# Joint input product of a hybrid diffusion step: heads in pairs, 256-column pieces, each part of a group summed in PSUM and added up afterwards

## The chip, the cores and the metric

One core of a Trainium2 chip runs the whole program. The metric is the device time of one execution in microseconds (us), the median of the runs shown. Matrix products run on TensorE (PE; its weight loads are PEld), elementwise work on VectorE (DVE), ScalarE (ACT) and GpSimd (POOL); SyncE (SP) issues most loads. Sixteen DMA engines move the data between device memory and the on-chip memory SBUF; PE writes only into PSUM, which has eight banks of 512 float32 columns by 128 partitions here.

## The reference, cut to what matters

Two streams of 128 tokens each (context and latent) pass through two trunk layers of width 2048. Layer 0 normalises the tokens, shifts and scales them with `adaLN` vectors (a matrix-vector product with `w_ada`), and multiplies them with `w_in`; the first 3072 columns of the result are queries, keys and values of 8 attention heads, the next 3072 are three streams of a linear recurrence, and the last 448 are its low-rank inputs.

```python
sh1, sc1, g1, sh2, sc2, g2 = split(silu(c) @ w_ada[l] + b_ada[l], 6)
h = rmsnorm(x, norm_g[l, 0]) * (1.0 + sc1) + sh1
proj = h @ w_in                       # 2048 x (3*1024 + 3*1024 + 448)
qa, ka, va, rest = split(proj, [1024, 2048, 3072])
q = qa.reshape(b, t, 8, 2, 64) ...    # 8 heads, two maps of 64; k likewise, v 8 heads of 128
```

Attention, recurrence, output product, ConvFFN, the convolution layer and its ConvFFN follow, and are not touched by the change.

## The kernel before, in words

Every weight matrix is streamed once. A load (SP, issued from `emit_load`, L175) brings a piece of up to 1024 columns by 128 rows into one of 7 `raw` buffers; ACT copies it as the high part (L192) and DVE makes the low part (L194) into one of 4 slots of `wbt`; PE then multiplies three times per 128x128 tile (high by high, high by low, low by high), each time against 256 token columns. The buffers and slots are reused in order, so a load waits until an older piece has been split, and a split waits until PE has used an older slot. The 128 rows of one step are called kt; there are 16.

`gemm_joint` (L273) is the first product of the program, on the 8 heads (groups of q, k, v: 3 tiles of 128 columns, in the matrix 1024 columns apart) and the group "x" (448 columns, 4 tiles). It can't run over all 16 kt in one go, since the `adaLN` vectors of those rows (`sc1`, `sh1`) have to be computed first, from 33.5 MB of `w_ada`. So the 16 kt are cut into five parts of 2, 2, 4, 4 and 4 (`KS`, L388). While one part is multiplied, `fill_joint` (L920) hands out the steps of the `w_ada` product for the next part: loads at L412 and small PE products at L431 (512 KB, 16 products each). `rhs_joint` makes the normalised, modulated rows `hbt` (L582, L585, L587) when a part's vectors are done. The load stream, `w_ada` and `w_in` together, is one queue on SP in the order of the program; PE, DVE and ACT work their lists in order too. A scheduler that models the engines sets these lists when the program is built.

Within a part, the first three heads (`NJ` = 3, `pl`) go piece by piece with 9 products per kt, and their 9 tiles stay in 5 PSUM banks over all five parts. The other five heads and the group x (`pl2`) are held: all pieces of a group are split first, and then each of its tiles is multiplied over the part's rows (L304 to L306), in one of the 2 remaining banks in turn; after each tile ACT (part 0, L309) or DVE (parts 1 to 4, L311) moves its 256 columns from PSUM into or onto the running sum in SBUF. A load of a head's pieces has three runs of 128 columns (512 bytes) per row and kt (L606), two kt to a piece of 768 columns.

After each group of the last part, `in_evac` queues that head's attention (`attn`), of which at most two are active and one step is taken per call of `step_tasks`; attention takes its PSUM banks from the same 7. Then `gemm(p_in, ...)` multiplies the remaining 3072 columns with the same stream (L252, L254, L255), with the rest of the attention in between, and the recurrence follows.

Of the kernel before, what the change touches and what calls it, by code (L numbers as in the profile page):

```python
# [10 lines left out]
F32 = mybir.dt.float32  # L11
# [3 lines left out]
ALU = mybir.AluOpType  # L15
# [4 lines left out]
P = 128  # L20
# [62 lines left out]
def tile_step(ctx: ExitStack, tc: tile.TileContext, A):  # L83
# [189 lines left out]
    def gemm_joint(pls, rhs, evac, sums, fill, steps=2):  # L273


        nts = [len(g["tiles"]) for g in pls[0][0].groups]
        banks = [bank() for _ in range((sum(nts) + 1) // 2)]
        pst = [banks[t // 2][:, (t % 2) * TT:(t % 2) * TT + TT] for t in range(sum(nts))]
        for pi, (pl, pl2) in enumerate(pls):
            last = pi == len(pls) - 1  # L280
            for gi, g in enumerate(pl.groups):
                t0 = sum(nts[:gi])
                for ki, kt in enumerate(pl.kts):
                    r = rhs(kt)
                    w = next_sub()
                    for j, off in enumerate(g["tiles"]):
                        hi, lo = w[:, 0, off:off + P], w[:, 1, off:off + P]
                        ps = pst[t0 + j]
                        pe.matmul(ps, lhsT=hi, rhs=r[:, 0:TT], start=(pi == 0 and ki == 0 and (t0 + j) % 2 == 0),
                                  stop=False, skip_group_check=True)  # L290
                        pe.matmul(ps, lhsT=hi, rhs=r[:, TT:2 * TT], start=False, stop=False, skip_group_check=True)
                        pe.matmul(ps, lhsT=lo, rhs=r[:, 0:TT], start=False, stop=(last and ki == len(pl.kts) - 1),
                                  skip_group_check=True)
                    pump(steps)
                    fill(pi)
                if last:
                    pending.append(evac(gi, g, pst[t0:t0 + nts[gi]]))
            for gi, g in enumerate(pl2.groups):
                rw = [(rhs(kt), next_sub(LA - i, i > 0)) for i, kt in enumerate(pl2.kts)]
                for j, off in enumerate(g["tiles"]):  # L300
                    ps = bank()[:, 0:TT]
                    for i, (r, w) in enumerate(rw):
                        hi, lo = w[:, 0, off:off + P], w[:, 1, off:off + P]
                        pe.matmul(ps, lhsT=hi, rhs=r[:, 0:TT], start=(i == 0), stop=False, skip_group_check=True)  # L304
                        pe.matmul(ps, lhsT=hi, rhs=r[:, TT:2 * TT], start=False, stop=False, skip_group_check=True)  # L305
                        pe.matmul(ps, lhsT=lo, rhs=r[:, 0:TT], start=False, stop=(i == len(rw) - 1),  # L306
                                  skip_group_check=True)
                    if pi == 0:
                        act.activation(sums[gi][j], ps, AF.Copy)  # L309
                    else:  # L310
                        dve.tensor_tensor(out=sums[gi][j], in0=sums[gi][j], in1=ps, op=ALU.add)  # L311
                    pump(steps)
                    fill(pi)
                if last:
                    pending.append(evac(gi, g, sums[gi]))
# [297 lines left out]
    for h in range(HA):  # L613
        g_in.append(grp([h * P, 1024 + h * P, 2048 + h * P], P, [0, P, 2 * P], kind="qkv", h=h))
# [4 lines left out]
    NJ = 3  # L619
    NQ = HA + 1  # L620
    w_in_view = view_for(A["w_in"][0])
    p_joint = [[Plan(w_in_view, gs, list(range(k0, k0 + n))) for gs in (g_in[0:NJ], g_in[NJ:NQ])] for k0, n in zip(K0, KS)]
# [29 lines left out]
    plans.extend([pl for pls in p_joint for pl in pls] + [p_in] + p_outs + p_f0 + [p_p1, p_p2] + p_f1)  # L652
# [46 lines left out]
    def mixer(hb, pjs):  # L699
# [49 lines left out]
        qkvs = [vb[:, 0:3], vb[:, 3:6], kk[:, 4:7]]  # L749
        qkvs += [qkvp.tile([P, 3, TT], F32, name=f"qkv{h}") for h in range(3, HA)]  # L750
        sums = [[qkvs[h][:, j] for j in range(3)] for h in range(NJ, HA)] + [[kk[:, j] for j in range(4)]]
# [114 lines left out]
        def in_evac(gi, g, pst):  # L866
            if g["kind"] == "qkv":
                qkv = qkvs[g["h"]]
                if g["h"] < NJ:
                    for j, ps in enumerate(pst):  # L870
                        act.activation(qkv[:, j], ps, AF.Copy)
                        yield
                tasks.append(attn(g["h"], qkv))
                return
            outs = []
# [939 lines left out]
```

## Time and profile before

| | |
|---|---|
| median of three runs | 2709.16 us (2708.67 to 2729.94) |
| profiled execution, own time | 2707.69 us |
| its span | 2705.6 us |
| granted TensorE clock, mean | 0.977 of full speed |
| PE, DVE, ACT, POOL busy | 97%, 75%, 47%, 11% of the span |
| DMA | 616.59 MB, mean 228 GB/s |
| joint product: first and last matmul | 36.7 and 269.0 us |
| product after it (`p_in`): first matmul | 269.1 us |

The page's rows give busy time by engine and line. A matmul's row lasts longer than its slot on PE, since matmuls are pipelined: what one costs is the step from its start to the next start. The view of windows sums each engine over a stretch and gives the granted clock and the DMA engines' busy share; the view of DMA gives packets, bytes and share by queue; the view of waits says for whom an engine sat idle.

### The profile page before, as it was taken

What the parts mean: (1) busy time and instruction counts of PE and PEld (TensorE: products, weight loads), DVE (VectorE), ACT (ScalarE), POOL (GpSimd) and SP (SyncE); (2) the same over time, 40 slices, a digit from 0 to 9 for tenths busy, and PEclk for the clock granted to TensorE, in tenths of its full rate; (3) what the DMA queues carried; (4) which work ended last, traced back from release to release, by engine and by line L of the source; (5) the groups of instructions that cost most, each with busy time, mean ns of one, the idle gap of its engine ahead of it and who ended that gap; (6) DMA issues with size and microseconds to landing.
All of it is one profiled execution on the core that took longest, in us unless ns stands there. A gap on an engine that the chain in (4) does not pass through costs nothing.

```text
span 2705.6 us, 60522 instructions
## 1 busy us (share of the span) xinstructions
PE 2615.6 (97%) x24347; PEld 2443.4 (90%) x24347; DVE 2020.5 (75%) x3468; ACT 1258.5 (47%) x2074; POOL 298.7 (11%) x313
## 2 busy tenths in 40 slices
PE   6999998999999999999999989999999999999998
PEld 5889996667898999999999989978889999999998
DVE  3457765767579998978999989996479985566655
ACT  3335654554345444434444454346344454355544
POOL 2000012011100000000000047653200000000000
PEclk8999999999799999999999989999999999999999
DMA  9997656655356887877878857865798876666653
GB/s 293 304 272 209 204 169 217 243 193 199 129 189 195 257 268 240 286 249 247 277 247 267 274 169 246 275 229 177 243 299 277 258 234 195 195 195 193 194 190 119
DMA packets 446969, 616.59 MB, mean 228 GB/s; under 512 B 33461, under 2 KB 317464, under 8 KB 446048
## 3 DMA queue, kind: packets, MB, share of 16 engines
q1 hardware_dynamic: 442288, 600.83, 70.2%
q0 software_dynamic: 3040, 6.57, 0.7%
q10 hardware_dynamic: 1360, 5.33, 0.5%
q8 instruction: 191, 3.13, 0.5%
q14 instruction: 90, 0.74, 0.1%
HBM read 604.75 MB, written 7.86 MB: 226 GB/s over the span
## 4 chain that ended last, share of the span: by engine, by line
PE 84%; DVE 7%; DMA 6%; ACT 1%; issue 1%; SPq 0%; POOL 0%; DVEq 0%; ACTq 0%; POOLq 0%
PE mm L255 22%; PE mm L252 22%; PE mm L254 22%; PE ada L431 4%; DVE cu L1655 3%; DMA raw<-in_w_ada 2%; DMA raw<-in_w_in 2%; PE mm L1087 1%; DVE wbt L194 1%; DMA raw<-in_w_up 1%; PE mm L304 1%; PE mm L306 1%; PE mm L305 1%; PE mm L1648 1%; PE mm L1120 1%
## 5 line engine op out<-in xcount | busy, mean ns | idle before, releaser
L192 ACT ACTIVATE wbt<-raw 128x1024 fp32r<-128x1024 f32 (+3 forms) x768 | 793.7, 1037 | 1035.4 <-PE mm L254 696.8
L252 PE MATMUL mm<-hbt,wbt 128*128 128x256 f32 x3888 | 1086.5, 282 | 6.0 <-ACT hbt L585 2.3
L254 PE MATMUL mm<-hbt,wbt 128*128 128x256 f32 x3888 | 1081.5, 280 | 2.7 <-DVE hbt L587 2.7
L194 DVE TENSOR_TENSOR wbt<-raw,wbt 128x1024 fp32r<-128x1024 f32 (+1 forms) x688 | 812.6, 1188 | 357.7 <-ACT wbt L192 345.5
L255 PE MATMUL mm<-hbt,wbt 128*128 128x256 f32 x3888 | 1064.2, 280 | 3.5 <-DVE wbt L194 3.3
L252 PEld LDWEIGHTS mm<-hbt,wbt 128*128 128x128 f32 x3888 | 733.3, 189 | 20.3 <-issue 9.2
L254 PEld LDWEIGHTS mm<-hbt,wbt 128*128 128x128 f32 x3888 | 734.0, 189 | 6.9 <-DVE hbt L587 4.7
L255 PEld LDWEIGHTS mm<-hbt,wbt 128*128 128x128 f32 x3888 | 723.2, 189 | 9.7 <-DVE wbt L194 4.7
L254 PE MATMUL mm<-u,wbt 128*128 128x256 f32 x1344 | 371.0, 278 | 0.0
L252 PE MATMUL mm<-u,wbt 128*128 128x256 f32 x1344 | 370.9, 278 | 0.0
L255 PE MATMUL mm<-u,wbt 128*128 128x256 f32 x1344 | 365.7, 278 | 0.0
L456 DVE SCALAR_TENSOR_TENSOR av<-raw,silu_c,av 128x1024 f32<-128x1024 f32 x270 | 337.2, 1278 | 29.6 <-DMA raw<-in_w_ada 29.5
L194 POOL TENSOR_TENSOR wbt<-raw,wbt 128x1024 fp32r<-128x1024 f32 x80 | 193.5, 2427 | 909.8 <-DMA raw<-in_w_pw 800.2
L252 PEld LDWEIGHTS mm<-u,wbt 128*128 128x128 f32 x1344 | 252.2, 188 | 0.4 <-issue 0.4
L254 PEld LDWEIGHTS mm<-u,wbt 128*128 128x128 f32 x1344 | 252.0, 188 | 0.4 <-issue 0.4
L255 PEld LDWEIGHTS mm<-u,wbt 128*128 128x128 f32 x1344 | 249.1, 188 | 0.4 <-issue 0.4
L431 PE MATMUL ada<-raw,silu_c 128*32 128x256 f32 (+2 forms) x2688 | 166.0, 337 | 31.3 <-DMA raw<-in_w_ada 15.6
L1655 DVE SCALAR_TENSOR_TENSOR cu<-mm,vec,cu 128x256 f32<-128x256 f32 x428 | 174.4, 470 | 2.2 <-ACT cu L1639 1.0
L1544 DVE SCALAR_TENSOR_TENSOR cv<-mm,vec,cv 128x254 f32<-128x254 f32 x344 | 147.3, 474 | 11.8 <-ACT cv L1539 11.8
L431 PEld LDWEIGHTS ada<-raw,silu_c 128*32 128x32 f32 x2688 | 70.3, 112 | 91.7 <-issue 26.2
L304 PE MATMUL mm<-hbt,wbt 128*128 128x256 f32 x304 | 91.7, 302 | 1.9 <-DVE qkv L311 1.0
L1539 ACT ACTIVATE cv<-mm,vec 128x256 f32<-128x256 f32 x172 | 72.0, 474 | 45.9 <-PE mm L255 45.8
(449 smaller groups left out, 2889.6 us busy)
## 6 DMA issues: line engine op xcount, KB each, us to landing
raw<-in_w_ada SPq DMA_DIRECT2D x384, 512.0 KB, 5.3
raw<-in_w_up SPq DMA_DIRECT2D x688, 256.0 KB, 4.2
raw<-in_w_down SPq DMA_DIRECT2D x168, 512.0 KB, 5.0
raw<-in_w_pw SPq DMA_DIRECT2D x128, 256.0 KB, 4.3
raw<-in_w_in SPq DMA_DIRECT2D x128, 192.0 KB, 6.1
raw<-in_w_in SPq DMA_DIRECT2D x48, 512.0 KB, 3.9
raw<-in_w_out SPq DMA_DIRECT2D x32, 512.0 KB, 4.0
raw<-in_w_pw SPq DMA_DIRECT2D x32, 512.0 KB, 4.7
```

Source lines behind the costliest of these rows:

```text
L192: act.activation(w[:, 0, 0:na * n], v, AF.Copy)
L194: pl.lo(pl.count).tensor_tensor(out=w[:, 1, 0:na * n], in0=v, in1=w[:, 0, 0:na * n].bitcast(F32), op=ALU.subtract)
L252: pe.matmul(ps, lhsT=hi, rhs=r[:, 0:TT], start=(ki == 0 and (nl > 0 or j % 2 == 0)), stop=False, skip_group_check=True)
L254: pe.matmul(ps, lhsT=hi, rhs=r[:, TT:2 * TT], start=False, stop=False, skip_group_check=True)
L255: pe.matmul(ps, lhsT=lo, rhs=r[:, 0:TT], start=False, stop=(ki == nk - 1), skip_group_check=True)
L304: pe.matmul(ps, lhsT=hi, rhs=r[:, 0:TT], start=(i == 0), stop=False, skip_group_check=True)
L305: pe.matmul(ps, lhsT=hi, rhs=r[:, TT:2 * TT], start=False, stop=False, skip_group_check=True)
L431: pe.matmul(ps[32 * j:32 * j + 32, 0:nb * 32], lhsT=silu_c[:, kt, :], rhs=rv[:, j], start=(kt == 0), stop=(kt == KT - 1))
L456: dve.scalar_tensor_tensor(out=av[:, s], in0=raw, scalar=sc, in1=av[:, s], op0=ALU.mult, op1=ALU.add)
L1539: act.activation(o, ps, AF.Copy, scale=w(1, ct))
L1544: dve.scalar_tensor_tensor(out=o[:, :, a_], in0=v2(ps)[:, :, b_], scalar=w(k, ct), in1=o[:, :, a_], op0=ALU.mult, op1=ALU.add)
L1655: dve.scalar_tensor_tensor(out=o, in0=pads[a](k), scalar=V("w_dw", k * KT + ct), in1=o, op0=ALU.mult, op1=ALU.add)
```

## The change

Heads are taken in pairs: a group is q, k and v of two heads, 3 runs of 256 columns (1 KB), 768 columns and 6 tiles; a piece holds one kt of such a group instead of two kt of one head. There are 4 pairs and the group x, all treated alike. A group takes 3 banks (x takes 2), is multiplied kt by kt over the part's rows with 18 products per piece, and at the part's end its banks are copied by ACT (part 0) or added by DVE (parts 1 to 4) in whole banks of 512 columns, except that heads 2 and 3 go in halves of 256, because their sums lie in different buffers. The heads' sums are laid out anew (two neighbouring heads side by side for q, for k and for v), and no tile stays in PSUM from part to part. `fill_joint` is called twice per piece, and its rate is set to that count. Two heads' attention is queued when a pair is done.

```diff
-    def gemm_joint(pls, rhs, evac, sums, fill, steps=2):
-        nts = [len(g["tiles"]) for g in pls[0][0].groups]
-        banks = [bank() for _ in range((sum(nts) + 1) // 2)]
-        pst = [banks[t // 2][:, (t % 2) * TT:(t % 2) * TT + TT] for t in range(sum(nts))]
-        for pi, (pl, pl2) in enumerate(pls):
-            last = pi == len(pls) - 1
+    def gemm_joint(pls, rhs, evac, sums, fill, steps=1):
+        for pi, pl in enumerate(pls):
             for gi, g in enumerate(pl.groups):
-                t0 = sum(nts[:gi])
+                nt = len(g["tiles"])
+                banks = [bank() for _ in range(nt // 2)]
                 for ki, kt in enumerate(pl.kts):
                     r = rhs(kt)
                     w = next_sub()
                     for j, off in enumerate(g["tiles"]):
                         hi, lo = w[:, 0, off:off + P], w[:, 1, off:off + P]
-                        ps = pst[t0 + j]
+                        ps = banks[j // 2][:, (j % 2) * TT:(j % 2) * TT + TT]
...
+                        if j in (nt // 2 - 1, nt - 1):
+                            pump(steps)
+                            fill(pi)
-            for gi, g in enumerate(pl2.groups):
-                rw = [(rhs(kt), next_sub(LA - i, i > 0)) for i, kt in enumerate(pl2.kts)]
-                for j, off in enumerate(g["tiles"]):
-                    ps = bank()[:, 0:TT]
...
-                    if pi == 0:
-                        act.activation(sums[gi][j], ps, AF.Copy)
-                    else:
-                        dve.tensor_tensor(out=sums[gi][j], in0=sums[gi][j], in1=ps, op=ALU.add)
-                    pump(steps)
-                    fill(pi)
+                for bk_, parts in zip(banks, sums[gi]):
+                    o = 0
+                    for t in parts:
+                        n = t.shape[-1]
+                        src = bk_[:, o:o + n]
+                        o += n
+                        if pi == 0:
+                            act.activation(t, src, AF.Copy)
+                        else:
+                            dve.tensor_tensor(out=t, in0=t, in1=src, op=ALU.add)
+                if pi == len(pls) - 1:
+                    pending.append(evac(gi, g, [t for parts in sums[gi] for t in parts]))
...
-    for h in range(HA):
-        g_in.append(grp([h * P, 1024 + h * P, 2048 + h * P], P, [0, P, 2 * P], kind="qkv", h=h))
+    for h in range(0, HA, 2):
+        g_in.append(grp([h * P, 1024 + h * P, 2048 + h * P], 2 * P, [P * j for j in range(6)], kind="qkv", h=h))
...
-    NJ = 3
-    NQ = HA + 1
+    NQ = HA // 2 + 1
...
-                qkv = qkvs[g["h"]]
-                if g["h"] < NJ:
-                    for j, ps in enumerate(pst):
-                        act.activation(qkv[:, j], ps, AF.Copy)
-                        yield
-                tasks.append(attn(g["h"], qkv))
+                tasks.extend(attn(h, qkvs[h]) for h in (g["h"], g["h"] + 1))
...
-                    want = (seen[pi][0] * 8 * KS[pi + 1]) // (NJ * KS[pi] + 19)
+                    want = (seen[pi][0] * 8 * KS[pi + 1]) // (2 * NQ * KS[pi])
```

What this does to the engines' lists is shown at three places. The first is SP's queue in the second half of the joint product (`raw` is the load buffer). Before:

```order
L606 DMA raw<-in_w_in 128x3x128 x2
L412 DMA raw<-in_w_ada 128x2x512 x2
L606 DMA raw<-in_w_in 128x3x128 x2
L412 DMA raw<-in_w_ada 128x2x512 x2
L606 DMA raw<-in_w_in 128x3x128 x2
```

and now:

```order
L402 DMA raw<-in_w_ada 128x2x512 x2
L596 DMA raw<-in_w_in 128x3x256
L402 DMA raw<-in_w_ada 128x2x512
L596 DMA raw<-in_w_in 128x3x256
L402 DMA raw<-in_w_ada 128x2x512 x2
L596 DMA raw<-in_w_in 128x3x256 x2
```

One issue of 384 KB stands where two of 192 KB stood; the mix of `w_ada` and `w_in` and its order stay much the same.

The second is PE around the last product of `w_ada` for this stage (`ada`; `mm` is a PSUM bank, `hbt` the rows, `wbt` the split weights). Before:

```order
L304 MATMUL mm_2421<-hbt_380,wbt_98 128x256
L431 MATMUL ada_2205<-raw_2384,silu_c_77 32x128 x8
L305 MATMUL mm_2421<-hbt_380,wbt_98 128x256
L306 MATMUL mm_2421<-hbt_380,wbt_98 128x256
L304 MATMUL mm_2421<-hbt_380,wbt_98 128x256
L305 MATMUL mm_2421<-hbt_380,wbt_98 128x256
L306 MATMUL mm_2421<-hbt_380,wbt_98 128x256
L304 MATMUL mm_2435<-hbt_380,wbt_98 128x256
```

and now:

```order
L289 MATMUL mm_2251<-hbt_381,wbt_98 128x256
L421 MATMUL ada_2181<-raw_2358,silu_c_77 32x128 x8
L286 MATMUL mm_2249<-hbt_381,wbt_98 128x256
L288 MATMUL mm_2249<-hbt_381,wbt_98 128x256
L289 MATMUL mm_2249<-hbt_381,wbt_98 128x256
L286 MATMUL mm_2249<-hbt_381,wbt_98 128x256
L288 MATMUL mm_2249<-hbt_381,wbt_98 128x256
L289 MATMUL mm_2249<-hbt_381,wbt_98 128x256
L286 MATMUL mm_2250<-hbt_381,wbt_98 128x256
```

The three lines of a tile's products are now L286, L288 and L289, and each bank comes back for every kt of the group. Of the 1344 products of the joint stage 485 stood behind this last `w_ada` product before, and 474 do now.

The third is DVE in the fourth part (rows of `wbt` are splits of pieces, the others add a bank of PSUM to a sum). Before:

```order
L194 TENSOR_TENSOR wbt_98<-raw_2259,wbt_98 128x768
L311 TENSOR_TENSOR qkv3_444<-qkv3_444,mm_2264 128x256
L311 TENSOR_TENSOR qkv3_444<-qkv3_444,mm_2288 128x256
L311 TENSOR_TENSOR qkv3_444<-qkv3_444,mm_2312 128x256
L194 TENSOR_TENSOR wbt_98<-raw_2336,wbt_98 128x768
L194 TENSOR_TENSOR wbt_98<-raw_2341,wbt_98 128x768
```

and now:

```order
L194 TENSOR_TENSOR wbt_98<-raw_2252,wbt_98 128x768
L194 TENSOR_TENSOR wbt_98<-raw_2294,wbt_98 128x768
L194 TENSOR_TENSOR wbt_98<-raw_2336,wbt_98 128x768
L194 TENSOR_TENSOR wbt_98<-raw_2368,wbt_98 128x768
L303 TENSOR_TENSOR qkv4_445<-qkv4_445,mm_2249 128x512
L303 TENSOR_TENSOR qkv4_445<-qkv4_445,mm_2250 128x512
```

Adds now come once per group and part, in whole banks. Here three pieces of the next pair (2294, 2336 and 2368) are split ahead of them. Over the 19 ends of groups at which another follows in this stage, two or three later pieces stand split ahead of the first add at 17, and one at 2.

## Rows read from the trace of the kernel before

**Rows 1.** The page, part 1: busy us (share of the span) xinstructions.
```profile
PE 2615.6 (97%) x24347; PEld 2443.4 (90%) x24347; DVE 2020.5 (75%) x3468; ACT 1258.5 (47%) x2074; POOL 298.7 (11%) x313
```

**Rows 2.** Windows of 0 to 450 us; the columns are named in the first row.
```profile
core 0: us, PE busy (x) PEld busy (x) DVE busy (x) ACT busy (x) POOL busy (x), PEclk, DMA share, GB/s
36.00:200.00 164.00, 156.76 (x1893) 134.73 (x1883) 77.49 (x166) 51.58 (x88) 0.00 (x0) 0.97 0.94 289
...
210.00:220.00 10.00, 10.00 (x88) 9.84 (x87) 5.58 (x10) 3.04 (x4) 0.00 (x0) 1.00 0.65 177
200.00:269.00 69.00, 65.27 (x526) 62.99 (x527) 54.51 (x130) 38.85 (x86) 4.99 (x8) 0.98 0.72 207
269.00:427.00 158.00, 158.00 (x1341) 154.30 (x1343) 100.61 (x190) 84.08 (x166) 21.35 (x51) 1.00 0.62 181
```

**Rows 3.** DMA of 36 to 200 us: queue's packets, MB, share of 16 engines; issues.
```profile
q1 hardware_dynamic: 51455, 47.12, 93.7%
...
raw<-in_w_ada SPq DMA_DIRECT2D x53, 512.0 KB, 6.3
raw<-in_w_in SPq DMA_DIRECT2D x84, 192.0 KB, 6.5
```

**Rows 4.** DMA of 210 to 220 us, heads' pieces alone.
```profile
q1 hardware_dynamic: 3550, 1.74, 64.2%
...
raw<-in_w_in SPq DMA_DIRECT2D x10, 192.0 KB, 3.3
```

**Rows 5.** DMA of 2350 to 2400 us, the second layer's `w_up` alone.
```profile
q1 hardware_dynamic: 10045, 9.68, 63.8%
...
raw<-in_w_up SPq DMA_DIRECT2D x38, 256.0 KB, 3.2
```

**Rows 6.** DMA of 2500 to 2550 us, the same loads.
```profile
q1 hardware_dynamic: 11384, 9.54, 63.4%
```

**Rows 7.** PE timeline about the last `w_ada` product: start us, us, engine, instruction.
```profile
199.08 0.28 PE L304 MATMUL mm<-hbt,wbt 128*128 128x256 f32 x1
199.29 0.65 PE L431 MATMUL ada<-raw,silu_c 128*32 128x128 f32 x16
199.86 0.39 PE L305 MATMUL mm<-hbt,wbt 128*128 128x256 f32 x1
```

**Rows 8.** PE timeline at the end of the joint product.
```profile
268.90 0.28 PE L305 MATMUL mm<-hbt,wbt 128*128 128x256 f32 x1
269.01 0.28 PE L306 MATMUL mm<-hbt,wbt 128*128 128x256 f32 x1
269.12 0.28 PE L252 MATMUL mm<-hbt,wbt 128*128 128x256 f32 x1
```

**Rows 9.** PE waits, 36 to 270 us: us in total, times, longest us.
```profile
PE ada L431 <- DMA raw<-in_w_ada: 5.3, 3, 2.6
PE mm L816 <- DVE a L810: 3.6, 1, 3.6
PE mm L304 <- DVE qkv L311: 1.0, 2, 0.7
PE mm L304 <- ACT qkv L309: 0.5, 1, 0.5
```

**Rows 10.** DVE lines by form, 0 to 270 us: count, busy us, mean ns, idle before.
```profile
L194 DVE TENSOR_TENSOR wbt<-raw,wbt 128x768 fp32r<-128x768 f32 x64 | 60.5, 954 | 61.6 <-ACT wbt L192 59.7 <-DMA raw<-in_w_in 1.9
L311 DVE TENSOR_TENSOR qkv<-qkv,mm 128x256 f32<-128x256 f32 x60 | 24.4, 415 | 26.1 <-PE mm L306 25.8
...
L1504 DVE COPY kb<-mm 128x512 f32<-128x512 f32 x4 | 2.6, 680 | 0.0
...
L371 DVE COPY vec<-mm 128x256 f32<-128x256 f32 x2 | 0.8, 398 | 0.0
```

**Rows 11.** PE timeline at the one long gap behind 200 us.
```profile
238.09 0.28 PE L306 MATMUL mm<-hbt,wbt 128*128 128x256 f32 x1
241.99 0.45 PE L816 MATMUL mm<-table,a 128*128 128x128 f32 x1 [3.62 <-DVE a L810]
...
244.15 0.41 PE L304 MATMUL mm<-hbt,wbt 128*128 128x256 f32 x1
244.37 0.41 PE L305 MATMUL mm<-hbt,wbt 128*128 128x256 f32 x1
```

More of the change, by code (lines that the diff above doesn't have):

```diff
@@ L287, in gemm_joint @@
                         hi, lo = w[:, 0, off:off + P], w[:, 1, off:off + P]
-                        ps = pst[t0 + j]
-                        pe.matmul(ps, lhsT=hi, rhs=r[:, 0:TT], start=(pi == 0 and ki == 0 and (t0 + j) % 2 == 0),
-                                  stop=False, skip_group_check=True)
+                        ps = banks[j // 2][:, (j % 2) * TT:(j % 2) * TT + TT]
+                        pe.matmul(ps, lhsT=hi, rhs=r[:, 0:TT], start=(ki == 0 and j % 2 == 0), stop=False,
+                                  skip_group_check=True)
@@ L291, in gemm_joint @@
                         pe.matmul(ps, lhsT=hi, rhs=r[:, TT:2 * TT], start=False, stop=False, skip_group_check=True)
-                        pe.matmul(ps, lhsT=lo, rhs=r[:, 0:TT], start=False, stop=(last and ki == len(pl.kts) - 1),
+                        pe.matmul(ps, lhsT=lo, rhs=r[:, 0:TT], start=False, stop=(ki == len(pl.kts) - 1),
                                   skip_group_check=True)
-                    pump(steps)
-                    fill(pi)
-                if last:
-                    pending.append(evac(gi, g, pst[t0:t0 + nts[gi]]))
@@ L298, in gemm_joint @@
-            for gi, g in enumerate(pl2.groups):
-                rw = [(rhs(kt), next_sub(LA - i, i > 0)) for i, kt in enumerate(pl2.kts)]
-                for j, off in enumerate(g["tiles"]):
-                    ps = bank()[:, 0:TT]
[L302 to L307, printed above, removed]
-                    if pi == 0:
-                        act.activation(sums[gi][j], ps, AF.Copy)
-                    else:
-                        dve.tensor_tensor(out=sums[gi][j], in0=sums[gi][j], in1=ps, op=ALU.add)
[L312 to L315, printed above, removed]
+                        if j in (nt // 2 - 1, nt - 1):
+                            pump(steps)
+                            fill(pi)
@@ L618, in tile_step @@
             g_in.append(grp([j0 + q * 512], 512, [0, P, 2 * P, 3 * P], kind=nm, c=4 * q))
-    NJ = 3
-    NQ = HA + 1
+    NQ = HA // 2 + 1
     w_in_view = view_for(A["w_in"][0])
-    p_joint = [[Plan(w_in_view, gs, list(range(k0, k0 + n))) for gs in (g_in[0:NJ], g_in[NJ:NQ])] for k0, n in zip(K0, KS)]
+    p_joint = [Plan(w_in_view, g_in[0:NQ], list(range(k0, k0 + n))) for k0, n in zip(K0, KS)]
     p_in = Plan(w_in_view, g_in[NQ:], list(range(KT)))
@@ L651, in tile_step @@
     stream["stop"] = len(g_in) * KT
-    plans.extend([pl for pls in p_joint for pl in pls] + [p_in] + p_outs + p_f0 + [p_p1, p_p2] + p_f1)
+    plans.extend(p_joint + [p_in] + p_outs + p_f0 + [p_p1, p_p2] + p_f1)
     def v2(ap):
@@ L748, in mixer @@
         vec_task = [vectors()]
-        qkvs = [vb[:, 0:3], vb[:, 3:6], kk[:, 4:7]]
-        qkvs += [qkvp.tile([P, 3, TT], F32, name=f"qkv{h}") for h in range(3, HA)]
-        sums = [[qkvs[h][:, j] for j in range(3)] for h in range(NJ, HA)] + [[kk[:, j] for j in range(4)]]
+        flat = lambda ap: ap.rearrange("p a t -> p (a t)")
+        twos = [vb[:, 0:6]] + [qkvp.tile([P, 6, TT], F32, name=f"qkv{h}") for h in (4, 6)]
+        ones_ = [kk[:, 4:7], qkvp.tile([P, 3, TT], F32, name="qkv3")]
+        sums = [[[flat(t[:, 2 * j:2 * j + 2])] for j in range(3)] for t in twos]
+        sums.insert(1, [[t[:, j] for t in ones_] for j in range(3)])
+        sums.append([[flat(kk[:, 2 * j:2 * j + 2])] for j in range(2)])
+        twos = [t.rearrange("p (m h) t -> p m h t", h=2) for t in twos]
+        qkvs = [twos[0][:, :, 0], twos[0][:, :, 1]] + ones_ + [twos[1 + i // 2][:, :, i % 2] for i in range(4)]
         tasks = []
@@ L867, in in_evac @@
             if g["kind"] == "qkv":
-                qkv = qkvs[g["h"]]
-                if g["h"] < NJ:
-                    for j, ps in enumerate(pst):
-                        act.activation(qkv[:, j], ps, AF.Copy)
-                        yield
-                tasks.append(attn(g["h"], qkv))
+                tasks.extend(attn(h, qkvs[h]) for h in (g["h"], g["h"] + 1))
                 return
+            if g["kind"] == "x":
+                pst = [kk[:, j] for j in range(4)]
             outs = []
```

## The prediction

> **What bounds the kernel now.** The page's first part comes first: PE is busy for 97% of the span [rows 1], so a change that only moves work off other engines gains little, and the question is where PE waits or stands in for a wait. The change touches the joint product alone, so the next view is the table of windows around it [rows 2]. The reader is to see two stretches with different limits. From 36 us, where the first joint product starts, to 200 us the DMA engines are busy for 94% of the time at 289 GB/s; PE's 157 of 164 us busy are not PE at its peak, because a lone matmul's row is longer than its slot. From 200 to 269 us the DMA share drops to 0.72 and PE does 526 instructions in 65.3 of 69 us; it is behind and catches up. The stretch from 269 to 427 us, the rest of the input product, has PE busy throughout: whatever the joint product ends earlier, that stretch starts earlier, and nothing in it takes the time back.
>
> The timeline tells what separates the two stretches [rows 7]: the last `w_ada` product of the stage runs at 199.3 us, and behind it PE has 485 joint products to do by the order of its list. They end at 269.1 us [rows 8]. One product costs 10.00 / 88 = 0.114 us where PE has nothing else [rows 2], so 485 cost 55.3 us; the other 14 us are attention's products and one long gap [rows 11]. So the end of the joint product is (arrival of the last `w_ada` piece, set by DMA) + (products behind it, set by PE). I cost the change in these two terms.
>
> **Term 1, DMA up to 200 us.** The bytes are the same. What changes is the run: 512 bytes per packet become 1 KB. Before, the heads' pieces alone (210 to 220 us) moved 1.74 MB at a share of 64.2% [rows 4], which is 1.74 MB / (10 us x 0.642) = 271 GB/s per full share. The later `w_up` loads have just the form that the change gives to the heads, runs of 256 columns, with 9.68 MB in 10045 packets: 9.68 / (50 x 0.638) = 303 [rows 5], and again 9.54 / (50 x 0.634) = 301 GB/s [rows 6]. In 36 to 200 us there are 84 issues of 192 KB, 16.5 MB [rows 3]: 61 us of all 16 engines at 271, 55 us at 302. That is 6 us less work for a resource that is busy for 93.7% of the stretch [rows 3], and I take all of it: -6.0. Its ends are 0, if packets overlap so that the stretch moves at the same rate, and -16: the 6 us, and the 10 us (6.3% of 164) in which the DMA engines stood idle because the load queue waited for buffers.
>
> [...]
>
> **Term 2, PE behind the last `w_ada` product.** By the new order 474 joint products stand behind it instead of 485: 11 x 0.114 = -1.3 us. The number of heads whose attention is complete at the end of the joint product stays at two; one more head gets as far as its scores there, and that work leaves the next stretch, which is PE's as well: 0.
>
> **Banks.** Before, only two banks were left for the held groups, and PE waited for the evacuation: 1.0 us for DVE and 0.5 us for ACT [rows 9]. Now three banks of a group are emptied while a whole next group (36 or 72 products, 4.1 or 8.2 us) runs, and seven banks hold two groups. These waits go: -1.5; ends 0 and -1.5.
>
> **Adds and copies.** DVE had 76 adds of 256 columns at 415 ns [rows 10]: 31.5 us. Now it has 24 of these and 44 of 512. The trace has no such add; a copy from PSUM takes 398 ns for 256 columns and 680 for 512 [rows 10], so I take 415 + 280 = 0.69 us (ends 0.415 and 0.83, twice the short one). That makes 10.0 + 30.4 = 40 us, 9 us more. DVE is busy for 77 of 164 and 54 of 69 us [rows 2]; of the 9 us 2 fall into the last part. Beside idle time they cost 0, and without that cover 9. ACT's copies out of PSUM grow and shrink by a few us at 52 of 164 us busy: 0.
>
> **Issues and fill.** SP makes 64 issues fewer; its queue waits for buffers, not for itself: 0. The `w_ada` steps keep their pace (18 steps are due at 22.5 of 40 calls, where it was 17.4 of 31).
>
> **The gap at 238 us.** PE waited 3.6 us for attention's weights `a`, and the twelve products behind it went at half the clock, 0.22 us apart [rows 11]: about 5 us in all. In the new list the same transposes stand 72 products behind the scores, but two heads share DVE and ACT on the way. I expect a wait of like size: 0; ends -5 and +4, a second such wait.
>
> **Sum.** -6.0 - 1.3 - 1.5 = -8.8 us. The profiled execution took 2707.7 us; it would take 2698.9. The median of the runs is 2709.2, 1.5 more, so on it I forecast 2700 us.
>
> **The rivals.**
>
> *No gain on DMA.* If the packets' cost is hidden between the 16 engines, or the memory behind them is the limit (from 36 to 200 us 47.1 MB moved at 93.7%, which is 307 GB/s per full share with both sizes mixed [rows 3]), term 1 is 0. For it: the mixed stretch is no slower than `w_up` alone. Against: more than half of its bytes are 2 KB runs. It gives 2709.2 - 2.8 = 2706 us. [...]
>
> *Everything closes up.* The held groups kept two of four slots until their last tile; now each slot comes free after 18 products. If that also fills the DMA engines' idle 10 us, and the gap at 238 us goes, the sum is -16 - 1.3 - 1.5 - 5 = -24: 2685 us. For it: PE waited 5.3 us for `w_ada` [rows 9] while the load queue stood still. Against: the queue's order has hardly changed.
>
> *Slower: the adds stand in front of the splits.* DVE works in order. An add waits until PE ends a group, and with it every split behind it; a group's adds take 3 x 0.69 us and the next split 0.95 [rows 10], 3.0 us in all, against 19 x 0.415 spread over a part before. One split piece gives PE 18 x 0.114 = 2.05 us of work. It decides at 3.0 / 2.05 = 1.5 pieces ahead: with one, PE stands still for about 1 us at each of 20 ends, +19 - 8.8 = 2719 us; with none, +60 - 8.8 = 2760. The list has two or three at 17 of 19 ends, which speaks against; for it speaks that a split there is only in the list, and its piece may be late.
>
> The other way in which the change could fail to do what it says, runs that are cut to 512 bytes anyway, is excluded by the packets of `w_up` (964 bytes on average [rows 5]).
>
> **How the numbers follow.** Forecast 0.50, no gain on DMA 0.22, everything closes 0.16, slower 0.12. The likeliest case alone spans 2693 to 2704. The range reaches from 2684, one below the third case's value, to 2712, three above the median, and leaves out most of the slower case and the far tail of the third. 1% is 27 us, about what a measurement of this kernel can tell from no change. Under 2682 lies only a part of the third case, if the first 36 us gain too: 0.07. Over 2736 lies the slower case with hardly any piece ahead: 0.05. The rest, 0.88, is no change by that measure.
>
> **What would show it.** Term 1: the last `w_ada` product at about 193 us instead of 199.3, and the heads' loads alone at about 300 GB/s per full share. Term 2: about 69 us from it to the end of the joint product, less 1 to 3. Banks: no PE wait on L301 or L303. The slower rival: PE waits for L194 at the ends of groups, with L303 just before it on DVE. The forecast is wrong if the next stretch, 158 us before, changes by more than 3 us, or if the recurrence behind it, whose lists were built anew, moves by itself.

## The result, and the profile after

The changed kernel takes 2694.4 us (median of 20 runs, 2690.9 to 2710.6), the kernel before beside it 2718.1 us (20 runs, 2701.9 to 2740.4). The ratio is 0.991, with a 95% interval of 0.989 to 0.9931: a gain of 0.7 to 1.1%, about what a measurement of this kernel can tell from no change. The forecast was 2700, from 2684 to 2712.

The runs of the kernel before fall into two groups (9 of 2701.9 to 2709.8 us, 11 of 2716.5 to 2740.4), those of the changed one lie within 6 us in 19 of 20 cases, with one at 2710.6. Lower group against lower group it is 2705.2 against 2694.4 us, and the two profiled executions, 2707.7 and 2696.3, stand as far apart: 11 us, and it is these 11 that the traces can explain. The rest of the 24 us between the medians is how often the upper group comes; the last section returns to it.

The page after, first part, as [rows 1]:

```profile
PE 2599.1 (96%) x24347; PEld 2436.0 (90%) x24347; DVE 2031.0 (75%) x3460; ACT 1258.8 (47%) x2063; POOL 300.5 (11%) x313
```

The windows of [rows 2], now:

```profile
36.00:200.00 164.00, 161.32 (x2019) 143.89 (x2020) 99.80 (x199) 63.47 (x104) 0.00 (x0) 0.98 0.96 316
200.00:269.00 69.00, 63.22 (x497) 60.52 (x496) 53.32 (x127) 38.28 (x89) 6.21 (x10) 0.95 0.63 187
269.00:427.00 158.00, 153.47 (x1299) 147.41 (x1297) 97.43 (x184) 80.61 (x154) 28.09 (x66) 1.00 0.61 175
```

The gain shows in the first one: 316 GB/s where it was 289, and 126 more PE instructions in the same 164 us. Its DMA, to set beside [rows 3]:

```profile
q1 hardware_dynamic: 38576, 51.45, 95.2%
...
raw<-in_w_ada SPq DMA_DIRECT2D x53, 512.0 KB, 6.0
raw<-in_w_in SPq DMA_DIRECT2D x51, 384.0 KB, 5.8
```

There are a quarter fewer packets, 4.3 MB more, and a share of busy time that is hardly higher. It looks as if the longer runs had done it. The heads' pieces alone (200 to 210 us, [rows 4]) speak against that:

```profile
q1 hardware_dynamic: 1777, 1.74, 62.8%
```

1.74 MB / (10 us x 0.628) = 277 GB/s per full share, against 271 before and some 300 forecast. The timeline at the last `w_ada` product and at the end of the joint product (L252 is the next stretch's first), as [rows 7, 8], and at attention's transposes, as [rows 11]:

```profile
185.97 0.64 PE L421 MATMUL ada<-raw,silu_c 128*32 128x128 f32 x16
...
231.46 0.30 PE L810 MATMUL mm<-table,a 128*128 128x128 f32 x1
232.63 0.44 PE L810 MATMUL mm<-table,a 128*128 128x128 f32 x2 [0.88 <-DVE a L804]
237.85 0.45 PE L810 MATMUL mm<-table,a 128*128 128x128 f32 x1 [4.78 <-DVE a L804]
...
259.38 0.28 PE L252 MATMUL mm<-hbt,wbt 128*128 128x256 f32 x1
```

And the PE waits from 36 to 270 us, as [rows 9]:

```profile
PE ada L421 <- DMA raw<-in_w_ada: 10.6, 4, 9.2
PE mm L810 <- DVE a L804: 5.7, 2, 4.8
PE mm L286 <- ACT hbt L575: 0.4, 1, 0.4
PE mm L288 <- DVE hbt L577: 0.3, 1, 0.3
```

(The 9.2 us lie ahead of the first joint product.) The last `w_ada` product comes 13.3 us earlier, the stretch behind it is 3.6 us longer (73.4 where it was 69.8), and the remaining 2435 us of the span are 1.5 shorter: together the 11. (Two more traces of the kernel before, below, divide these 11 otherwise.)

### The profile page after: what moved, and what is told of

Read it like the earlier page. It is cut to its first block, busy times and chain, and to the rows that moved or that the text cites. A ratio compares the mean times of both kernels' runs of the same rounds, so it can differ in the third digit from the quotient of the medians.

```text
span 2694.4 us, 60352 instructions
## 1 busy us (share of the span) xinstructions
PE 2599.1 (96%) x24347; PEld 2436.0 (90%) x24347; DVE 2031.0 (75%) x3460; ACT 1258.8 (47%) x2063; POOL 300.5 (11%) x313
## 4 chain that ended last, share of the span: by engine, by line
PE 80%; DVE 5%; DMA 3%; ACT 1%; issue 1%; POOL 1%; SPq 1%; DVEq 0%; ACTq 0%; POOLq 0%
PE mm L252 22%; PE mm L255 22%; PE mm L254 22%; PE ada L421 3%; DMA raw<-in_w_ada 2%; PE mm L1078 1%; DMA raw<-in_w_up 1%; DVE cu L1646 1%; DVE wbt L194 1%; PE mm L1639 1%; PE mm L1111 1%; DVE av L446 1%; PE mm L1115 0%; PE ada L454 0%; PE mm L1273 0%
## 5 line engine op out<-in xcount | busy, mean ns | idle before, releaser
L252 PE MATMUL mm<-hbt,wbt 128*128 128x256 f32 x3888 | 1087.5, 282 | 6.0 <-ACT hbt L575 2.3
L254 PE MATMUL mm<-hbt,wbt 128*128 128x256 f32 x3888 | 1082.3, 280 | 3.2 <-DVE hbt L577 3.2
L194 DVE TENSOR_TENSOR wbt<-raw,wbt 128x1024 fp32r<-128x1024 f32 (+1 forms) x688 | 814.0, 1189 | 351.8 <-ACT wbt L192 343.1
L255 PE MATMUL mm<-hbt,wbt 128*128 128x256 f32 x3888 | 1065.1, 281 | 5.5 <-DVE wbt L194 5.3
L252 PEld LDWEIGHTS mm<-hbt,wbt 128*128 128x128 f32 x3888 | 734.3, 189 | 20.6 <-issue 9.2
L252 PE MATMUL mm<-u,wbt 128*128 128x256 f32 x1344 | 371.1, 278 | 0.0
L194 POOL TENSOR_TENSOR wbt<-raw,wbt 128x1024 fp32r<-128x1024 f32 x80 | 193.8, 2431 | 908.5 <-ACT wbt L192 905.7
L252 PEld LDWEIGHTS mm<-u,wbt 128*128 128x128 f32 x1344 | 252.2, 188 | 0.4 <-issue 0.4
L421 PE MATMUL ada<-raw,silu_c 128*32 128x256 f32 (+2 forms) x2688 | 157.3, 338 | 31.6 <-DMA raw<-in_w_ada 25.2
L286 PE MATMUL mm<-hbt,wbt 128*128 128x256 f32 x448 | 131.6, 298 | 0.4 <-ACT hbt L575 0.4
L288 PE MATMUL mm<-hbt,wbt 128*128 128x256 f32 x448 | 127.1, 285 | 0.3 <-DVE hbt L577 0.3
```

The source lines that it names most:

```text
L194: pl.lo(pl.count).tensor_tensor(out=w[:, 1, 0:na * n], in0=v, in1=w[:, 0, 0:na * n].bitcast(F32), op=ALU.subtract)
L252: pe.matmul(ps, lhsT=hi, rhs=r[:, 0:TT], start=(ki == 0 and (nl > 0 or j % 2 == 0)), stop=False, skip_group_check=True)
L255: pe.matmul(ps, lhsT=lo, rhs=r[:, 0:TT], start=False, stop=(ki == nk - 1), skip_group_check=True)
L286: pe.matmul(ps, lhsT=hi, rhs=r[:, 0:TT], start=(ki == 0 and j % 2 == 0), stop=False, skip_group_check=True)
L421: pe.matmul(ps[32 * j:32 * j + 32, 0:nb * 32], lhsT=silu_c[:, kt, :], rhs=rv[:, j], start=(kt == 0), stop=(kt == KT - 1))
```

## The experiments

The stretch up to the last `w_ada` product gained twice what I had given the longer runs. Four things had changed at once: the length of the runs, the slots that a held group kept, the pace of the `w_ada` steps, and the three heads that lay in PSUM over all parts. Each was taken by itself. "w_ada" and "joint" are the start of the last `w_ada` product and of the first product behind the joint ones, in us of the one trace; "layer" is the time from the start of the first product of the second layer's `w_down` to that of the last one. Each ratio is to the runs of the kernel before that were taken beside that kernel (their medians are 2714.6 to 2722.6 us in the series e1 to e10); it is not the quotient of two medians of the table.

| kernel | median us (runs) | ratio to before, 95% | w_ada | joint | layer |
|---|---|---|---|---|---|
| before, three traces | 2718.1 (20) | | 199.3, 195.8, 195.2 | 269.1, 265.8, 265.5 | 464.0 each |
| changed | 2694.4 (20) | 0.991, 0.989 to 0.9931 | 186.0 | 259.4 | 464.0 |
| e1 runs of 512 bytes | 2696.5 (7) | 0.9925, 0.9889 to 0.9961 | 186.0 | 259.6 | 464.0 |
| e2 single heads | 2693.5 (12) | 0.9912, 0.9886 to 0.9938 | 183.0 | 248.7 | 464.0 |
| e3 transposes later | 2690.3 (12) | 0.9918, 0.9885 to 0.9951 | 185.1 | 243.6 | 464.0 |
| e4 four heads | 2716.6 (12) | 0.9993, 0.997 to 1.0015 | 180.0 | 254.6 | 481.9 |
| e5 single, slots held | 2687.7 (10) | 0.9904, 0.9866 to 0.9942 | 185.6 | 251.7 | 464.0 |
| e6 before, six slots | 2737.7 (4) | 1.0108, 1.0047 to 1.0169 | 194.5 | 275.5 | 481.9 |
| e7 before, even pace | 2715.4 (10) | 1.0029, 0.9986 to 1.0072 | 197.3 | 269.3 | 464.0 |
| e8 before, none held | 2700.2 (10) | 0.9945, 0.9914 to 0.9976 | 185.0 | 249.7 | 481.9 |
| e9 as e5, transposes later | 2690.6 (12) | 0.9924, 0.989 to 0.9957 | 185.7 | 246.1 | 464.0 |
| e10 as e8, two banks left | 2729.7 (10) | 1.0051, 1.0009 to 1.0093 | 204.3 | 283.8 | 481.9 |

The cause is read from the columns w_ada and joint. The medians mix in the last column, which has two values 18 us apart, in code that no edit touches; what picks the value is not known.

**The runs.** In the changed kernel a piece is fetched by head:

```
+            if g.get("kind") == "qkv":
...
+                for i in range(2):
+                    eng.dma_start(out=d4[:, i], in_=s4[:, :, i * P:(i + 1) * P])
+                return
...
-        g_in.append(grp([h * P, 1024 + h * P, 2048 + h * P], 2 * P, [P * j for j in range(6)], kind="qkv", h=h))
+        g_in.append(grp([h * P, 1024 + h * P, 2048 + h * P], 2 * P, [(j % 2) * 384 + (j // 2) * P for j in range(6)], kind="qkv", h=h))
```

> The changed kernel with one thing undone: a pair's piece of 128x768 is fetched in two transfers of 192 KB with runs of 128 columns (512 bytes), one for each head, into a slot that holds the heads one behind the other. Loop order, sums, adds and slots stay. Theory A, the length of the runs: the load rate in the stretch that DMA limits falls back from 329 to about 304 GB/s per full DMA share (100 to 150 us), the last w_ada product comes at about 198 us instead of 186, the joint product ends at about 270 us instead of 259, and the time is about 2705 us, 11 above the changed kernel. Theory B, the structure (a part's group is finished before the next begins, so slots come free evenly): the last w_ada product stays at 186 to 188 us and the time at 2694 to 2697 us.

The DMA of 36 to 200 us and the last `w_ada` product of this kernel:

```profile
q1 hardware_dynamic: 58961, 51.48, 102.0%
...
raw<-in_w_in SPq DMA_DIRECT2D x102, 192.0 KB, 6.1
```

```profile
185.99 0.64 PE L421 MATMUL ada<-raw,silu_c 128*32 128x128 f32 x16
```

Half as many packets again, twice the issues of the heads, and the same bytes in the same time to 0.1%: theory A is out. The share of busy time rose from 95.2 to 102.0% and the last `w_ada` product started at 185.99 us against 185.97, so the share was not a measure of room left. That is what had misled me.

**Loop order and pairs.** The new `gemm_joint` with the old groups (`for h in range(HA)`, pieces of 128 columns, two rows a slot):

> The new loop order alone: heads one at a time as before (pieces of 128 columns, two rows of a head in a slot, runs of 512 bytes, adds of 512 and 256 columns), but every head goes through PSUM part by part and none is held over the parts. Theory A, the length of the runs: as before the change, last w_ada product at about 198 us, joint product to about 270 us, time about 2706 us. Theory B, the structure: last w_ada product at 186 to 188 us and about 2695 us. If the first experiment keeps the gain and this one loses it, it is the pairs' slot (one row of six tiles instead of two rows of three) and not the runs.

183.0 us with runs of 512 bytes: the gain needs neither the pairs nor the runs. The joint product even ends 10.7 us earlier than in the changed kernel, but the profiled execution, 2699.9 us, is 3.6 longer. Its windows (columns as in [rows 2]) show why:

```profile
560.00:570.00 10.00, 10.00 (x141) 7.11 (x140) 7.60 (x20) 6.51 (x17) 1.05 (x3) 0.77 0.46 164
570.00:580.00 10.00, 10.00 (x66) 6.54 (x61) 1.79 (x4) 2.08 (x3) 0.53 (x2) 0.50 0.22 59
580.00:590.00 10.00, 10.00 (x65) 8.43 (x64) 3.96 (x11) 3.33 (x5) 0.52 (x1) 0.50 0.59 206
590.00:600.00 10.00, 10.00 (x86) 6.25 (x84) 6.81 (x25) 6.34 (x17) 1.17 (x4) 0.87 0.48 162
```

In the recurrence the granted clock fell to 0.50 in this execution, by the four means for about 27 us; the lead was gone: from the first product behind the joint ones to the first of `w_out` this execution took 459.7 us, the changed kernel's 443.4. The traces of before and after show 1.00 in all four windows; a stretch at half clock comes later in both, with a mean of 0.57 from 680 to 720 us before and of 0.66 from 660 to 710 us after. Of e2's 12 runs the profiled one shows the lowest mean clock, 0.974, so this loss need not be in its median, 2693.5 us.

**Four heads to a group**, 512 columns and one transfer of 512 KB for each of q, k and v:

> The change carried on: q, k and v of four heads are a group each, 512 columns in one run of 2 KB, two rows in a slot, one transfer of 512 KB for a slot. Theory A, a cost per packet: if 1 KB runs brought 13 us against 512 bytes, 2 KB runs bring half as much again, 5 to 7 us; the last w_ada product at about 180 us and the time about 2688 us. Rival A2, nothing beyond 1 KB: 186 us and about 2694 us. Rival B, the structure: slots come free after 24 products and two rows, as with single heads before, so that DMA idles more: 188 to 192 us and about 2698 us. Attention starts later in the last part (four heads at a time); I cost that at nothing, since the next stretch covers it.

The 180.0 us that theory A named came, and yet e1 speaks against the runs as its source, and so does e2: product 672 of 1344, half of the joint ones, starts at 147.2 us here and at 148.1 with single heads and 512 bytes (151.0 in the changed kernel, 162 to 167 before). Of the 28 us by which this execution is longer than the changed kernel's, about 10 had been lost by the end of the recurrence, which begins 5 us earlier here but stands at half clock for some 22 us longer (59 us against 37, by the means of the windows of 434 to 715 us), and 18 in the second layer, the last column. The same window of the second layer in this kernel and in the changed one:

```profile
2300.00:2350.00 50.00, 50.00 (x427) 50.00 (x426) 23.57 (x26) 19.10 (x18) 0.00 (x0) 1.00 0.58 184
```

```profile
2300.00:2350.00 50.00, 50.00 (x444) 50.00 (x443) 26.95 (x35) 19.12 (x18) 0.00 (x0) 1.00 0.63 192
```

427 products in 50 us against 444, at a granted clock of 1.00 in both.

**The slots.** First, single heads with a group's products tile by tile over its rows, as before for five heads and x:

```
-                for ki, kt in enumerate(pl.kts):
-                    r = rhs(kt)
-                    w = next_sub()
-                    for j, off in enumerate(g["tiles"]):
+                rw = [(rhs(kt), next_sub(LA - i, i > 0)) for i, kt in enumerate(pl.kts)]
+                for j, off in enumerate(g["tiles"]):
+                    ps = banks[j // 2][:, (j % 2) * TT:(j % 2) * TT + TT]
+                    for ki, (r, w) in enumerate(rw):
```

> Single heads, part by part through PSUM, as in the second experiment, with one thing put back: a group's products go tile by tile over the part's rows, so that its two slots of four stay in use until its last tile (as the kernel before did for five heads and x; here all nine groups). Theory B1, held slots: with two of four slots held, DVE's split of the next pieces waits, the raw slots stay full and the load queue stands still; the last w_ada product goes back from 183 to 197 to 205 us, the joint product ends at 262 to 270 us instead of 249. Theory B2, the pace of the w_ada steps or the banks that the first three heads kept over all parts: held slots cost nothing, 183 to 186 us and 249 to 252 us.

Then the kernel before with `WB` 6 instead of 4 in this stage:

> The kernel before with six slots of split weights instead of four in the input product, and attention's heads one at a time with one set of buffers (to make room; attention starts behind 215 us, so up to there only the slots differ). Theory B1, held slots: held groups leave four slots for what comes next, so the last w_ada product comes at 186 to 190 us instead of 199. Theory B2: it stays at 197 to 200 us. What the joint product and the time do behind 215 us says nothing here, since attention takes longer by itself.

185.6 and 194.5 us: holding two slots costs 2.6 us against e2, less than the 4 us by which traces of one kernel differ, and six slots bring nothing beyond the 195 us of the other two traces of before. Held slots, the mechanism of my rival "everything closes up", are out as the cause.

**The pace** of the `w_ada` steps in the kernel before, by products (`n` is their number since the last call):

```
-                    seen[pi][0] += 1
-                    want = (seen[pi][0] * 8 * KS[pi + 1]) // (NJ * KS[pi] + 19)
+                    seen[pi][0] += n
+                    want = (seen[pi][0] * 8 * KS[pi + 1]) // (84 * KS[pi])
```

> The kernel before with the w_ada steps paced by joint products (84 a row of a part) instead of by calls of the filler, as even as in the changed kernel; PSUM, loop order, runs and slots stay. Theory B2a, the pace: the uneven pace lets DMA stand idle at 57 to 73 and 151 to 171 us; with an even one product 168 comes at 65 to 67 us instead of 71 to 73 and the last w_ada product at 186 to 189 us instead of 195 to 199. Theory B2b, the three heads held in PSUM over all parts, which leave two banks for five heads and x: nothing changes, 71 to 73 and 194 to 200 us.

197.3 us, and product 168, the first of the second part, at 72.4 (70.7 to 72.8 in the three traces of before, 65.3 after): the pace is out.

**The heads held in PSUM.** The kernel before with one number changed (and the divisor of `want` that follows from it):

```
-    NJ = 3
+    NJ = 0
```

> The kernel before with the number of heads held in PSUM over all parts set from three to none: all eight heads and x go tile by tile, one bank a tile, and seven banks rotate instead of two; runs of 512 bytes, slots and adds of 256 columns stay (45 adds more). The pace becomes even by itself. Theory B2b: product 168 at 64 to 67 us, the last w_ada product at 183 to 188 us, the joint product's end at 247 to 262 us. If only the pace counts, the same, and then the run with the even pace shows it too. If neither counts: 71 to 73 and 194 to 200 us; then only the layout of whole banks (two tiles to a bank, one copy or add for both) is left as the cause.

Product 168 at 66.1, the last `w_ada` product at 185.0, the joint product's end at 249.7: all of the gain, with 512-byte runs, old slots, old tile-by-tile loops and more adds.

```profile
185.01 0.64 PE L431 MATMUL ada<-raw,silu_c 128*32 128x128 f32 x16
...
249.67 0.28 PE L252 MATMUL mm<-hbt,wbt 128*128 128x256 f32 x1
```

Its counterpart takes the same kernel and lets five banks lie idle:

```
+        banks = [bank() for _ in range(5)]
+        for bk_ in banks:
+            pe.transpose(bk_[:, 0:P], ident, ident)
...
+        for i, bk_ in enumerate(banks):
+            tc.keep_in_program_order(dve.tensor_copy(junk[:, 0, i:i + 1], bk_[:, 0:1]))
```

> The kernel of the eighth experiment (no head held in PSUM over the parts) with one thing added: five of the seven banks are taken at the start of the joint product (a transpose of the identity into each) and freed at its end (a copy of one column each), so that two banks rotate as in the kernel before, while loop order, adds, runs and slots are those of the eighth. Theory B2b, the free banks: product 168 comes at 70 to 74 us instead of 66, the last w_ada product at 194 to 202 us instead of 185, the joint product's end 9 us later or more. Rival: it is the order of the first three heads (row by row over PSUM, without copies) that costs, and the number of banks does nothing: 65 to 68, 184 to 188 and 248 to 253 us.

Product 168 at 78.6, the last `w_ada` product at 204.3, the end at 283.8.

```profile
204.25 0.42 PE L436 MATMUL ada<-raw,silu_c 128*32 128x128 f32 x6
...
283.83 0.28 PE L252 MATMUL mm<-hbt,wbt 128*128 128x256 f32 x1
```

Two banks against seven, with nothing else changed but what ties the five up, is worth 19 us up to the last `w_ada` product. The times follow: the two profiled executions, both with 481.9 us in the last column, took 2737.5 and 2701.2 us. Holding three heads in the banks is no loss by itself: with two banks left, before, which holds them, has its last `w_ada` product at 195 to 199 us and e10, which holds none, at 204. So it is shown that the free banks are the cause. How they work is a reading of traces and lists, not tested further. The windows of the second half of the first part, from product 84 to product 168, in the kernel before and in e8:

```profile
53.40:72.60 19.20, 16.09 (x182) 14.00 (x179) 5.61 (x10) 7.65 (x17) 0.00 (x0) 0.91 0.88 262
```

```profile
54.90:66.00 11.10, 11.10 (x121) 10.54 (x118) 5.52 (x10) 8.39 (x22) 0.00 (x0) 1.00 1.08 323
```

Before, DMA moves 262 GB/s there against 323, and PE waits:

```profile
58.63 0.39 PE L304 MATMUL mm<-hbt,wbt 128*128 128x256 f32 x1 [0.54 <-ACT qkv L309]
...
62.67 0.64 PE L431 MATMUL ada<-raw,silu_c 128*32 128x128 f32 x16 [2.56 <-DMA raw<-in_w_ada]
```

and from 64 to 67 us, behind that wait, its products come 0.21 us apart at a granted clock of 0.50. PE's list suggests a reason for the second wait. With two banks the scheduler can't put a third tile behind the second until one is emptied, and it seems to fill the place with `w_ada` products: in the first part they break into the joint products 16 times in e10, mostly after 6 or 12 products, one tile or two, 13 times in before, 9 times in e8 and 8 times in the changed kernel. By this reading PE, with few banks, comes to a `w_ada` piece before it has landed and stands there, the splits behind it find no free slot, the load queue no free buffer, and DMA loses time that the stretch can't give back. In e10 PE waits 13 times for such pieces:

```profile
PE ada L436 <- DMA raw<-in_w_ada: 11.9, 13, 2.8
```

Two things in the traces leave this reading unproven. The first part holds only about half of the gain: e8 is 4.6 to 6.7 us ahead of the three traces of before at product 168, and 10.0 to 14.7 at product 672; behind the first part the lists differ little in this respect (48 places with `w_ada` products in before, 46 in e8, 44 in e10 and in the changed kernel). And the load queue's own waits from 36 to 180 us, 74 to 77 us in total in before, are 77 in e8, 86 in e10 and 103 in the changed kernel, so its last link doesn't show in that view. That the banks are worth these microseconds is shown; the way by which they are is open.

**The gap behind 231 us.** The changed kernel with the first two heads' transposes later:

```
-            yield
-            yield
+            for _ in range(12 if h < 2 else 2):
+                yield
```

> The changed kernel, with the transposes of attention's weights (PE L810) of the first two heads ten steps later: 228 joint products behind the scores instead of 72. Theory C: the two waits for DVE's a (0.9 and 4.8 us) stand on the path that sets the end; without them the joint product ends at about 253.5 us and the time falls by 5 to 6 us to about 2688 us. Rival: behind the last w_ada product PE is not alone the limit, and the load queue or DVE's splits take the time back; the joint product ends within 2 us of 259 and the time stays at 2694 us.

PE's waits from 36 to 270 us in this kernel:

```profile
PE ada L421 <- DMA raw<-in_w_ada: 10.0, 3, 9.5
PE mm L286 <- ACT hbt L575: 0.4, 1, 0.4
```

The joint product ends 15.8 us earlier, 10 more than theory C said, since attention's later steps go with the transposes into the next stretch (16 of its products lie between the last `w_ada` product and the end, where it was 50). The profiled execution takes 2689.8 us, 6.5 less than that of the changed kernel. That is the time theory C named, in one trace of each; the medians, 2690.3 and 2694.4, were taken in different sessions. The same on top of e5:

> Single heads with held slots and part-by-part sums, as in the fifth experiment (its median was 2688 us), with the first two heads' transposes of a ten steps later, as in the third. Theory C: the waits of 0.8 and about 1 us behind 219 us go, the joint product ends 1 to 3 us earlier and the time falls to about 2686 us. Rival: the lists of attention and of the recurrence behind it are built anew and move the time by as much either way; 2684 to 2692 us.

The joint product ended 5.6 us earlier, more than either theory said, and the medians, 2690.6 and 2687.7, don't tell the two apart. e3, e5 and e9 lie 4 to 7 us below the changed kernel by median, with intervals that overlap its own, and by the ratio to the runs beside them only e5 (0.9904) is below its 0.991: candidates, not a proven gain.

**The kernel before, twice more**, for a trace of its upper group:

> The kernel before, unchanged, for a second trace. Its runs lie in two groups, 2702 to 2710 and 2716 to 2740 us. In the traces so far 400 products of a stretch that is PE's alone take 47.1 us in some stretches and 45.3 in others at a granted clock of 1.00 in both, and the last 4300 products went at the shorter one in every kernel but the one with four heads to a group. Theory D: the upper group are runs in which the last 4300 products keep the longer one: +19 us there and nothing elsewhere; a trace of about 2725 us would show 47.1 us for 400 products behind 2200 us. Rival: the upper group comes from a lower granted clock in the recurrence (430 to 700 us), as 565 to 592 us at half the clock in the trace with single heads, about +12 us. A trace of about 2706 us shows neither.

> The same once more, since each run falls in either group about half the time. Theory D: about 2725 us with 47.1 us for 400 products behind 2200 us, or about 2706 us with 45.3. Rival: about 2718 us with a granted clock of about 0.5 somewhere between 430 and 700 us, and 45.3 us for 400 products at the end.

2708.1 and 2707.5 us: both fell in the lower group, with 464.0 us in the last column, so neither theory was tested. They are of use for the scatter: the last `w_ada` product of before comes at 195.2 to 199.3 us, so about 10 of the 13.3 us above are the change, and 3 to 4 that one execution; all three traces end level, with spans of 2705.4 to 2706.0 us. Measured from these two, the joint product ends only 6 us earlier in the changed kernel, and the other 5 of the 11 us come behind it: from there to the first product of `w_out` before's three traces take 446.3, 453.7 and 448.6 us, the changed kernel's 443.4. So the joint product holds 6 to 10 of the 11 us; whether the rest is the change or the scatter of the recurrence, one trace of the changed kernel can't tell.

## Why the prediction came out, and where it was wrong

The forecast was 5.6 us above the measured median and inside its range, and on the profiled execution 2698.9 against 2696.3. That is luck in good part: the term for the runs was worth nothing, the banks were worth several times their term, the gap cost 5 us, and the errors offset each other. As a difference of medians the forecast was -9 us and the measurement -24, and the value still fell into the range because the forecast started from three runs whose median, 2709.2 us, lay in the lower group of before.

*Which stretch.* Right: up to 200 us DMA set the pace (a share of 0.94 before and 0.96 after), the end of the joint product was the arrival of the last `w_ada` piece plus PE's work behind it, and the next stretch kept its length (154.5 us from the first product of the rest of the input product to its last, 155.4 before, inside the 3 us). The recurrence behind it, which the sum left as it was, moves by itself: by up to 7 us between traces of the unchanged kernel, as above.

*Term 1, -6.0 for the longer runs.* The stretch gained 9 to 13 us, and none through the runs: e1 measures that term at 0.0. The failed step is "6 us less work for a resource that is busy for 93.7%": it took bytes over busy share for a capacity. At 1 KB and at 512 bytes the same 51.5 MB went through at shares of 95.2 and 102.0%, 316 GB/s at either size. My 271 and 302 GB/s per full share came from stretches with shares of 64%; no row of before showed the two sizes each by itself at the 93.7% where I used them.

*Banks, -1.5, with ends of 0 and -1.5.* This is the term that was mis-sized. I priced the two banks at PE's recorded waits for L309 and L311 [rows 9], which did go to zero as forecast. e8 puts the banks at 10 to 14 us up to the last `w_ada` product, e10 at 19. The waits on the evacuation were the small end of it; the large one showed as waits for `w_ada` and as a lower DMA rate, by the reading above because of where the list puts the other work when a bank is missing.

*Term 2 and the gap.* 474 products stand behind, as counted, but the stretch became 3.6 us longer instead of 1.3 shorter. The gap "of like size" grew from 3.6 to 5.7 us of waits, and the granted clock of 200 to 269 us fell from 0.98 to 0.95; the 4.9 us of difference are just over the +4 that I had given it. e3 shows what was to be had there.

*Adds.* Right: the 512-column add takes the 0.69 us that I had estimated, and the 9 us more on DVE cost nothing that shows:

```profile
L303 DVE TENSOR_TENSOR qkv<-qkv,mm 128x512 f32<-128x512 f32 x24 | 16.0, 681 | 8.0 <-PE mm L289 8.0
```

*Rivals.* "No gain on DMA" had its premise (the runs bring nothing) right and its time wrong, because the banks stood in. "Everything closes up" had the size of the first stretch about right, -16 against -13, for a reason that e5 and e6 refute. The adds in front of the splits did not come about: no PE wait for L194 stands among those of 36 to 270 us.

## What to carry to other kernels

The price of a scarce buffer need not be the wait that is booked on it. Here 1.5 us were booked on the two banks, and freeing them was worth 10 and more, part of which stood as waits for other data; where a scheduler orders the lists anew, freeing the buffer, or tying it up on purpose, shows its worth directly. And bytes divided by a busy share were no capacity here (51.5 MB in 164 us at 95.2 and at 102.0%): before a faster load is put into a sum, the same loads belong in a saturated stretch at both sizes.

## What was not expected of the hardware

- A stream of the same products at a granted clock of 1.00 ran at one of two steady periods in these traces: 50 us / 427 = 0.117 us and 50 us / 444 = 0.113 us. Up to about 2180 us PE-bound stretches mostly go at the longer one in the traces of before and after (427 products in both from 1100 to 1150 us). The second layer, from its first `w_down` product to its last, takes 464.0 us in ten traces, among them three of before, and 481.9 in four (e4, e6, e8, e10), 18 us more. The medians of before's two groups of runs, 2705.2 and 2725.2 us, are about as far apart. In the series of 30 beside e1 to e4, its runs with a mean clock of 0.977 to 0.979 took 2705 to 2710 or 2720 to 2732 us. That the upper group is the longer period in the last layer is thus likely; no trace of before in that group was caught, and what chooses the period stays open. It may go with the built kernel as much as with the execution: all 10 runs of e8, whose trace has the longer one, lie within 9 us. If so, e8, which changes one number of before, would stand at about 2682 us with the shorter one, by an estimate from its median and these 18 us.
- The share of busy DMA time went over 100% (102.0% with 58961 packets in e1, 36 to 200 us) with no loss of rate (316 GB/s, as in the changed kernel at 95.2%).
- The additional half clock of some 27 us in the recurrence of e2 cost about half of that, 13 us, by an estimate from the clock alone; the recurrence took 16 us longer than in the changed kernel. That is more than the 11 us that the change brought between profiled executions.
